# A decoder layer on one core: the last passes of the first feed-forward join the mixing stage's list schedule, which gets other costs and ranks

## The chip, the cores and the metric

The kernel runs on one core of a Trainium2 chip. Its time is the device time of one execution in microseconds (us). Before the change it is 2037.16 us, the median of three runs (2036.92 to 2037.41). The engines are named as in the profile: PE is TensorE's matmul, PEld its weight load, DVE is VectorE, ACT is ScalarE, POOL is GpSimd, and SP is SyncE, whose queue issues all the transfers.

## The reference, cut to what matters

16 meta tokens stand before 1024 tokens of width 1024. One layer is a first half-step feed-forward, a mixing stage, and a second half-step feed-forward; a norm closes it.

```python
h = h + 0.5 * swiglu(rmsnorm(h, norm_ffn1), w_ffn1_gate, w_ffn1_up, w_ffn1_down)   # d_ff = 2816
u = rmsnorm(h, norm_mix)
qa, ka, va, qi, ki, wi, qs, ksw, vsw, ga, gb = split(u @ w_in)      # rope on all q and k
score = sum_h relu(qi_h . ki) * wi_h                                # 4 index heads
o_sparse = softmax attention over each query's 256 best keys by score   # 8 heads, one k and v
o_swa = softmax attention over a window of 128 keys, with sinks         # 8 heads, two k and v
merged = sigmoid(ga) * (o_sparse @ w_bs) + sigmoid(gb) * (o_swa @ w_bw)
h = h + merged @ w_out
h = h + 0.5 * swiglu(rmsnorm(h, norm_ffn2), ...)
out = rmsnorm(h[tokens], norm_final)
```

## The kernel before, in words

Everything is held with the model width on the partitions and the tokens along the row, in two halves: half 0 has 528 columns (the meta tokens and 512 tokens), half 1 has 512. float32 products are made of float16 ones: each operand is split into a high and a low float16 part, and three matmuls are summed. A weight comes by a DMA into one of two staging buffers (`wst`), ACT writes its high part and DVE its low part into one of four buffers (`wsp`), and PE reads those. `split_w` is that pair of instructions.

A feed-forward works through the inner width in four groups. The first three groups, and the gate and up products of the fourth, are written out by hand with a fast scheme for 2 x 2 blocks. What is left, the down product of the fourth group, runs as two **plain passes**: for half 0 and then half 1, each of eight output rows `d` takes one weight, matmuls into the PSUM tile `pdn`, an addition into `h[d]` by DVE, a square by ACT (`sq`) and an addition into `acc` by DVE. After a pass, `norm_stats` (PE tile `nsum`, then a few DVE steps on `n_a`, `n_r`, `n_e`) and `norm_u` (PE tile `nbc`, then for each `d` the DVE product `un`, an ACT copy and a DVE subtraction, both into `u`) make the mixing stage's input. Half 0's norm is done during half 1's pass. `h` is also written out to DRAM, as `hspill`, to be read again at the end of the mixing stage.

The mixing stage is recorded and not executed at once: the class `Plan` collects its instructions, and `run` simulates the five queues with a cost per instruction and writes each engine's order out. At each step it takes the engine that can start first and, among that engine's ready instructions, the one with the lowest rank; the rank is the place in the recorded program plus `nc.shift`. The engines then execute that order strictly, each in its own queue, whatever the real durations are. The names in it: `rp` and `rt`, `ry` are the rope projections and their products; `kscr`, `qscr` are their way through DRAM into the stacked `k` and `q`; `pv_t` is the projection of the values; `ps_i`, `rel` and `sc1` to `sc7` are the index scores of the query blocks; `ps_s`, `psw`, `ptr`, `pts`, `pv_s`, `otr`, `oT` belong to the window attention; MAX8 and MATCH_REPLACE8 on `sc` and `m8` find the 256 best in blocks 1 to 4, and a binary search (`jk`, `s5...`) does so for blocks 5 to 7; `ps_a`, `psp`, `ptb`, `pv_b` are the sparse attention; `p_gate`, `p_br`, `gt`, `mg` the gates and branch products; `p_out` the output product.

Before the change the plan starts after the plain passes (`nc.start()` stands behind the call of `ffn`), so its first entries are half 1's norm and the rope projections. The cost of a DVE instruction in the plan depends on its width alone; a POOL instruction that runs beside it changes nothing.

Of the kernel before, what the change touches and what calls it, by code (L numbers as in the profile page):

```python
# [117 lines left out]
        return self.made  # L118


def overlap(a, b):
    return a is None or b is None or all(x0 < y1 and y0 < x1 for (x0, x1), (y0, y1) in zip(a, b))

# [9 lines left out]
class Plan:  # L133
# [48 lines left out]
    def add(self, engine, op, args, kw):  # L182
        if not self.on:
            give = lambda x: x.get() if isinstance(x, View) else x
            return getattr(engine.real, op)(*[give(a) for a in args], **{k: give(v) for k, v in kw.items()})  # L185
        outs = [a for a in args[:1]] + [kw[k] for k in ("out", "accum_out") if k in kw]
        ins = list(args[1:]) + [v for k, v in kw.items() if k not in ("out", "accum_out")]
        outs = [o for o in outs if isinstance(o, View)]
        ins = [o for o in ins if isinstance(o, View)]
        i = len(self.items)  # L190
        busy, done = self.cost(engine.name, op, outs, ins)
        if engine.name == "ACT" and "accum_out" in kw:
            busy, done = busy + 0.1, done + 0.19
        deps, new = set(), []
        for views, write in ((ins, False), (outs, True)):
            for v in views:
                b, box = v.base, v.box()
                for j, other, wrote in b.seen:
                    if (write or wrote) and j != i and overlap(box, other):
                        deps.add(j)  # L200
                if write and box is None:
                    b.seen = []
                b.seen.append((i, box, write))
                if b.first is None:
                    b.first = i
# [5 lines left out]
        self.items.append((engine, op, args, kw, busy, done, deps, new, i + self.shift))  # L211

    def start(self):
        self.on = True

    def run(self, keep=(), margin=0.25):
        items, names = self.items, ("PE", "DVE", "ACT", "POOL", "SP")
        count = len(items)
        kept = {id(t.base) for t in keep}
# [6 lines left out]
        for i, it in enumerate(items):  # L226
            for j in it[6]:
                users[j].append(i)
            waits[i] = len(it[6]) + len(it[7])
            for b in it[7]:  # L230
                queues.setdefault(b.key, []).append((i, b))
                free.setdefault(b.key, [0.0] * b.bufs)
# [13 lines left out]
        wire = [0.0]  # L246
        order, when = [], [0.0] * count

        def settle(i):
# [19 lines left out]
        while len(order) < count:  # L269
            best = None  # L270
            for e in names:
                while future[e] and future[e][0][0] <= clock[e]:
                    _, p, i = heapq.heappop(future[e])
                    heapq.heappush(now[e], (p, i))
                if now[e]:
                    t = clock[e]
                elif future[e]:
                    t = future[e][0][0]
                else:
                    continue  # L280
# [12 lines left out]
            order.append(i)  # L293
            for j in users[i]:
                f = items[j][0].name
                lag = 0.04 if f == e else 0.07 + (margin if f == "PE" else 0.0)
                at = t if f == e == "PE" else end + lag
                ready[j] = max(ready[j], at)
                waits[j] -= 1
                if not waits[j]:  # L300
                    settle(j)
            for b in dies[i]:
                if b.key in free:
                    free[b.key].append(end + 0.1)
                    grant(b.key)
# [26 lines left out]
def layer_kernel(ctx: ExitStack, tc: tile.TileContext, xT, gains, wgu1, wd1, win, wvi, wbs, wbw, wout,  # L332
# [24 lines left out]
        return new(big, [P, 528], F32, tag="nt", name=name, bufs=2)  # L357

    def tmp(shape, dt, name):
        return new(ph["sb"], shape, dt, tag="t", name=name, bufs=6)  # L360

    def atmp(shape, dt, name):
        return new(ph["sb"], shape, dt, tag="ta", name=name, bufs=2)

    def mcst(shape, dt, name, bufs=1):
        return new(ph["sb"], shape, dt, tag=name, name=name, bufs=bufs)
# [49 lines left out]
    def load_w(src, n, st=None):  # L416
        if st is None:
            st = load_raw(src, n)
        sp = wsp_tile()
        split_w(sp, st, n)  # L420
        return sp

    def mm3(ps, w, wcols, xt, xcols, start, stop):
# [49 lines left out]
        return res  # L473

    def fpage(shape, dt, name):
        return new(ph["sb"], shape, dt, tag="fp", name=name, bufs=27)

    def ftmp(name):
        return new(ph["sb"], [P, 528], F32, tag="ft", name=name, bufs=6)
# [23 lines left out]
                nc.scalar.activation(rb[:, s0:s1], ps[:, :w], AF.Copy)  # L503
        return (u, rb) if keep else u

    def ffn(u, rb, hs, gi, wgu, wd, other_half, passes, saved):
        S = ph["S"]
        wa = hs[0][0].shape[1] // S
        wb = 512 // S
# [7 lines left out]
        def new_hid(x):  # L517
            made[0] += 1
            shape = [P, 2, hs[x][0].shape[1]]
            if made[0] <= 11:  # L520
                return fpage(shape, F16, "hid")
            if made[0] <= 19:
# [301 lines left out]
        with tc.manual_schedule(engines=ORDERED):  # L824
            for f0, f1 in F_GROUPS:
# [23 lines left out]
                if not last:  # L849
                    for d in range(0, KD, 2):  # L850
                        fast_down(d, down)
        ready = None
        for x, subs, done in passes:
            c0, c1 = subs[0][0], subs[-1][1]
# [2 lines left out]
            for d in range(KD):  # L857
                nd = (f1 - f0) * P
                w = load_w(wd[d // 2][:, 2 * f0 * P + d % 2 * nd:2 * f0 * P + (d % 2 + 1) * nd], nd)
                ps = wide("pdn")  # L860
                if full:
                    plain(ps, w, [t[x] for t in hid], x)
# [44 lines left out]
    acc = ffn(u1, rb1, h, 0, wgu1, wd1, lambda: ffn1_norm(1),  # L907
              ((0, SUB_ALL[0], lambda r: mix_norm(0, r)), (1, SUB_ALL[1], None)), saved1)
    close_phase()
    open_phase("mix")  # L910
    nc.start()

    cos, sin = [], []
    for lst, i in ((cos, 0), (sin, 1)):
# [369 lines left out]
    for x in range(2):  # L1284
# [10 lines left out]
        for b in range(4 * x, 4 * x + 4):  # L1295
            swa_block(b, qs, oT_w[x])
    qa += q_groups((0, 1), 8, 2)

    vm_sp = v_meta(lambda hh: 0)
    oT_s = [new_oT()]  # L1300
# [102 lines left out]
    acc = ffn(u3, rb3, h2, 2, wgu2, wd2, lambda: ffn2_norm(1, acc), passes, saved2)  # L1403
    x, subs, done = passes[-1]
    done(norm_stats(acc, subs))
    close_phase()
# [91 lines left out]
```

## Time and profile before

| | us |
|---|---|
| median of three runs | 2037.16 |
| the profiled execution | 2036.95 |
| its span | 2035.0 |
| PE busy in the span | 1928.4 |
| DVE busy | 1627.0 |
| ACT busy | 900.8 |
| POOL busy | 385.7 |

The span has three parts that can be told apart in PE's rows: the first feed-forward to 637.89 us (the first matmul of the plain passes), the plain passes and the mixing stage to 1386.4 us, and the second feed-forward after that. An engine's busy time is a union: two instructions that overlap at their ends count once. The durations of single rows are a little longer than the distance from one start to the next, for the same reason. "PEclk" is the clock that TensorE was granted, as a share of 2.4 GHz.

### The profile page before, as it was taken

How to read it: one execution, taken by the hardware profiler on the slowest of the kernel's cores; microseconds unless marked ns; L12 is line 12 of the kernel's file. 1: busy time of each engine (PE TensorE's matmuls, PEld its weight loads, DVE VectorE, ACT ScalarE, POOL GpSimd, SP SyncE). 2: the span in 40 equal slices, each digit the busy share in tenths (PEclk: the TensorE clock that was granted, in tenths of full speed). 3: DMA queues.
4: the chain of work that ended last, by engine and by line, in shares of the span. 5: the costliest groups of instructions: out<-in, count | busy, mean ns of one | idle time of the engine just before them, and what ended most of it. 6: DMA issues, size and time to landing. Idle time of an engine off the chain costs nothing.

```text
span 2035.0 us, 32861 instructions
## 1 busy us (share of the span) xinstructions
PE 1928.4 (95%) x13080; PEld 1202.6 (59%) x13080; DVE 1627.0 (80%) x2779; ACT 900.8 (44%) x1602; POOL 385.7 (19%) x313
## 2 busy tenths in 40 slices
PE   5899999999999688889999999998899999999997
PEld 3488888888888354555555656444344444444443
DVE  7888788778875859999997977566988787788767
ACT  4433233333323434578888555443433243233232
POOL 3511312221310024122000000002312212312200
PEclk9899999999999799999999999999999999999998
DMA  4011111111113444321111232241112121111213
GB/s 158 11 63 48 58 63 51 55 63 58 48 63 101 135 142 140 95 84 58 34 46 33 74 103 73 83 156 52 32 57 65 46 75 49 63 62 47 76 39 129
DMA packets 58873, 146.95 MB, mean 72 GB/s; under 512 B 7264, under 2 KB 13408, under 8 KB 58720
## 3 DMA queue, kind: packets, MB, share of 16 engines
q1 hardware_dynamic: 58720, 144.86, 22.4%
q8 instruction: 102, 1.67, 0.3%
q14 instruction: 51, 0.42, 0.1%
HBM read 130.01 MB, written 14.76 MB: 71 GB/s over the span
## 4 chain that ended last, share of the span: by engine, by line
PE 75%; DVE 14%; ACT 5%; issue 3%; DMA 2%; POOL 1%; SPq 0%; DVEq 0%; ACTq 0%; POOLq 0%
PE pc L185 15%; PE pd L185 14%; PE pa L185 14%; PE pb L185 7%; PE p_gate L312 7%; PE p_out L312 4%; PE p_br L312 4%; PE pdn L185 3%; DVE sc L312 2%; PE ptr L312 2%; DVE u L185 1%; ACT psw L312 1%; PE pv_b L312 1%; PE rp L312 1%; ACT jk L312 1%
## 5 line engine op out<-in xcount | busy, mean ns | idle before, releaser
L185 PEld LDWEIGHTS <-wsp 128*128 128x128 f16 x5136 | 506.8, 99 | 312.0 <-issue 35.5
L185 PEld LDWEIGHTS <-x 128*128 128x128 f16 x3132 | 306.4, 98 | 156.4 <-issue 7.8
L312 PEld LDWEIGHTS <-wsp 128*128 128x128 f16 x2160 | 207.1, 98 | 205.6 <-ACT wsp L312 6.1
L185 PE MATMUL pa<-u,wsp 128*128 128x264 f16 (+1 forms) x1440 | 224.7, 310 | 0.0
L312 PE MATMUL p_gate<-u,wsp 128*128 128x512 f16 x768 | 187.3, 379 | 0.0
L185 POOL TENSOR_TENSOR h<-h,base 128x512 f32<-128x512 f32 (+1 forms) x72 | 116.3, 1616 | 291.1 <-DVE base L185 229.7
L185 ACT ACTIVATE wsp<-wst 128x1024 f16<-128x1024 f32 (+2 forms) x104 | 90.4, 870 | 165.8 <-DMA wst<-in_wd_dram 60.3
L312 PE MATMUL rp<-u,wsp 128*128 128x512 f16 (+2 forms) x624 | 143.4, 367 | 9.0 <-ACT wsp L312 5.8
L312 DVE SCALAR_TENSOR_TENSOR wsp<-wst,wsp 128x1024 f16<-128x1024 f32 (+1 forms) x88 | 98.1, 1116 | 32.9 <-ACT wsp L312 32.8
L185 PE MATMUL pb<-tb,wsp 128*128 128x264 f16 (+1 forms) x720 | 114.0, 312 | 7.9 <-ACT tb L185 5.7
L185 PE MATMUL pc<-tb,x 128*128 128x264 f16 (+1 forms) x720 | 112.3, 310 | 5.9 <-DVE c L185 5.7
L185 PE MATMUL pc<-tb,wsp 128*128 128x256 f16 (+1 forms) x720 | 114.8, 315 | 0.0
L312 ACT ACTIVATE wsp<-wst 128x1024 f16<-128x1024 f32 (+1 forms) x88 | 81.2, 928 | 70.1 <-PE p_out L312 23.7
L185 PE MATMUL pd<-u,x 128*128 128x256 f16 (+1 forms) x720 | 110.7, 308 | 0.0
L185 PE MATMUL pd<-tb,x 128*128 128x256 f16 (+1 forms) x720 | 110.7, 308 | 0.0
L185 DVE SCALAR_TENSOR_TENSOR wsp<-wst,wsp 128x1024 f16<-128x1024 f32 (+2 forms) x104 | 104.8, 1008 | 7.2 <-ACT wsp L185 7.1
L185 ACT ACTIVATE wsp<-sa 128x1024 f16<-128x1024 f32 (+1 forms) x64 | 62.3, 973 | 103.3 <-DVE sa L185 103.2
L185 POOL TENSOR_TENSOR t<-g,g 128x512 f32<-128x512 f32 x16 | 25.2, 1576 | 434.6 <-DVE g L185 434.6
L312 ACT ACTIVATE jk<-sc,s5nb 128x784 f16<-128x784 f32 (+2 forms) x93 | 98.4, 1058 | 16.0 <-DVE s5nb L312 13.5
L185 PE MATMUL pa<-hid,wsp 128*128 128x264 f16 (+1 forms) x648 | 103.1, 310 | 0.0
L185 PE MATMUL pd<-hid,x 128*128 128x256 f16 (+1 forms) x648 | 101.6, 308 | 0.0
L185 DVE TENSOR_TENSOR c<-pc,base 128x512 f32<-128x512 f32 x80 | 55.4, 692 | 51.6 <-PE pc L185 51.3
(215 smaller groups left out, 3442.3 us busy)
## 6 DMA issues: line engine op xcount, KB each, us to landing
wst<-in_wgu_dram SPq DMA_DIRECT2D x88, 512.0 KB, 3.9
wst<-in_win_dram SPq DMA_DIRECT2D x44, 512.0 KB, 3.5
wst<-in_wd_dram SPq DMA_DIRECT2D x48, 384.0 KB, 3.5
wst<-in_wd_dram SPq DMA_DIRECT2D x32, 256.0 KB, 2.7
wst<-in_wout_dram SPq DMA_DIRECT2D x16, 512.0 KB, 3.9
qscr<-ry SPq DMA_DIRECT2D x20, 256.0 KB, 2.1
q<-qscr SPq DMA_DIRECT2D x20, 256.0 KB, 3.1
wst<-in_wbs_dram SPq DMA_DIRECT2D x16, 256.0 KB, 2.9
```

The costliest lines, as they stand in the source:

```text
L185: return getattr(engine.real, op)(*[give(a) for a in args], **{k: give(v) for k, v in kw.items()})
L312: getattr(engine.real, op)(*[give(a) for a in args], **{k: give(v) for k, v in kw.items()})
```

## The change

Six things are edited. The plain passes of the first feed-forward are recorded into the plan (a callback, `to_mix`, closes the first phase, opens the mixing phase and starts the plan before the passes); in that form half 0 is two PSUM tiles, of 272 and 256 columns, and not one. The hidden tiles that the passes read move to a pool that outlives the phase and is shared with the mixing stage's temporary tiles. The plan adds 0.4 us to a DVE instruction that has two float32 inputs in SBUF and none in PSUM while a POOL instruction other than a copy is still running, and 1.3 us to an ACT instruction that needs another function table than the last. SP may start 6 us ahead of the plan's zero, and a transfer lands 0.5 us later in it. The weight splits get a rank that is 300 lower. And the projections of the window attention's queries are recorded between the index scores of two query blocks and those of the next two, those of the sparse attention's queries between and after the window blocks of half 1.

```diff
-    def run(self, keep=(), margin=0.25):
+    def run(self, keep=(), margin=0.25, early=0.0):
...
-            engine, op, args, kw, busy, done, deps, new, _ = items[i]
+            engine, op, args, kw, busy, done, deps, new, _, shared = items[i]
+            if e == "DVE" and shared and pool_till > t:
+                busy, done = busy + 0.4, done + 0.4
+            elif e == "ACT" and len(args) > 2 and args[2] in TABLES:
+                if TABLES[args[2]] != table:
+                    table = TABLES[args[2]]
+                    busy, done = busy + 1.3, done + 1.3
...
+            if e == "POOL" and op != "tensor_copy":
+                pool_till = end
...
-                end = wire[0] + 0.7
+                end = wire[0] + 1.2
...
         sp = wsp_tile()
+        nc.shift = -300
         split_w(sp, st, n)
+        nc.shift = 0
...
+        before_passes()
         ready = None
         for x, subs, done in passes:
...
+                if ph["mix"]:
+                    for a, b in subs:
+                        ps = mmps("pdn")[:, :b - a]
+                        proj(ps, w, [t[x] for t in hid], a, b)
+                        hv = hs[x][d][:, a:b]
+                        nc.vector.scalar_tensor_tensor(hv, ps, DS, hv, op0=ALU.mult, op1=ALU.add)
+                    square_into(d, hs[x][d], acc)
...
+                    if ready and d == 0:
+                        r = norm_stats(*ready[:2])
+                    if ready and d == 1:
+                        ready[2](r)
+                    continue
...
+    def to_mix():
+        close_phase()
+        open_phase("mix")
+        nc.start()
...
-        for b in range(4 * x, 4 * x + 4):
-            if b:
-                score(b)
-        qs += q_groups((x,), 4, 2)
...
+        first = 4 * x
+        scores((first, first + 1))
+        half = q_groups((x,), 4, 1)
+        scores((first + 2, first + 3))
+        qs.append(half[0] + q_groups((x,), 6, 1)[0])
...
-    nc.run(h2[0] + h2[1] + u3[0] + rb3 + [acc])
+    nc.run(early=6.0, keep=h2[0] + h2[1] + u3[0] + rb3 + [acc])
```

The instructions themselves stay the same but for the narrower pieces of half 0; what changes is the order. Three places show it. The first is PE at the end of the plain passes (`pdn` of `h[7]` of half 1 is the last piece of them; `nsum` and `nbc` are half 1's norm; `rp1` is the first rope projection of half 0). Before:

```order
L185 MATMUL pdn_7647<-hid_7100,wsp_7644 128x512
L312 MATMUL nsum_7674<-ones_97,acc_7384 128x1 x4
L312 MATMUL nbc_7717<-ident_93,n_r_7701 128x128 x4
L312 LDWEIGHTS wsp_7754
L312 MATMUL rp1_7761<-u_7445,wsp_7754 128x272
```

and now:

```order
L326 LDWEIGHTS wsp_7629
L326 MATMUL pdn_7669<-hid_7100,wsp_7629 128x512
L326 LDWEIGHTS wsp_7674
L326 MATMUL rp1_7693<-u_7534,wsp_7674 128x272
L326 LDWEIGHTS wsp_7674
```

Half 1's norm no longer stands between the passes and the rope projection; its `nsum` now comes behind four further projections. The second place is DVE at the same point: the low part of the first rope weight (`wsp_7754` before, `wsp_7674` now). Before it comes behind six products of half 1's norm (`un` of `h_77` to `h_82`):

```order
L312 SCALAR_TENSOR_TENSOR un_7725<-h_77,g_all_95,nbc_7717 128x512
L312 SCALAR_TENSOR_TENSOR un_7728<-h_78,g_all_95,nbc_7717 128x512
L312 TENSOR_TENSOR u_7731<-un_7725,u_7731 128x512
...
L312 SCALAR_TENSOR_TENSOR un_7756<-h_82,g_all_95,nbc_7717 128x512
L312 SCALAR_TENSOR_TENSOR wsp_7754<-wst_7711,wsp_7754 128x1024
```

and now it comes before the last addition of the passes (`h_84`), while half 1's `acc` additions follow among the rope products:

```order
L326 SCALAR_TENSOR_TENSOR wsp_7674<-wst_7619,wsp_7674 128x1024
...
L326 SCALAR_TENSOR_TENSOR h_84<-pdn_7669,h_84 128x512
L326 SCALAR_TENSOR_TENSOR wsp_7702<-wst_7650,wsp_7702 128x1024
...
L326 SCALAR_TENSOR_TENSOR wsp_7766<-wst_7697,wsp_7766 128x1024
L326 TENSOR_TENSOR acc_7477<-acc_7477,sq_7779 128x512
L326 TENSOR_TENSOR rt2_7805<-rp2_7733,cs_7137 128x272
```

So the weight's split has moved ahead of half 1's norm, and the norm's DVE work has moved behind the first rope products. The third place is SP's queue ahead of the plain passes (`wd1` holds their weights, `wgu1` the last gate and up weights). Before, six weights of the passes stand in a row:

```order
L185 DMA wst_6611<-in_wgu1_dram 128x1024
L185 DMA wst_7112<-in_wd1_dram 128x512
L185 DMA wst_7146<-in_wd1_dram 128x512
L185 DMA wst_7180<-in_wd1_dram 128x512
L185 DMA wst_7214<-in_wd1_dram 128x512
L185 DMA wst_7248<-in_wd1_dram 128x512
```

and now the masks stand behind the second:

```order
L188 DMA wst_6611<-in_wgu1_dram 128x1024
L326 DMA wst_7125<-in_wd1_dram 128x512
L326 DMA wst_7131<-in_wd1_dram 128x512
L326 DMA msk0_7141<-in_m_swa0_dram 128x144
L326 DMA msk1_7143<-in_m_swa_dram 128x256
L326 DMA sp0_7145<-in_m_sp0_dram 128x144
L326 DMA snk_7147<-in_sinks_dram 128x8
L326 DMA wst_7160<-in_wd1_dram 128x512
```

The mask's transfer goes into memory of the closed phase, so it waits for the last DVE instruction of that phase, and the third weight stands behind it.

## Rows read from the trace of the kernel before

**Rows 1.** The page's first part: busy time of each engine, share, instructions.

```profile
PE 1928.4 (95%) x13080; PEld 1202.6 (59%) x13080; DVE 1627.0 (80%) x2779; ACT 900.8 (44%) x1602; POOL 385.7 (19%) x313
```

**Rows 2.** Windows: busy us and instructions by engine, then PEclk, DMA share, GB/s.

```profile
637.89:688.00 50.11, 46.64 (x310) 30.47 (x307) 40.13 (x81) 24.14 (x47) 0.11 (x1) 0.97 0.54 176
688.00:706.00 18.00, 5.08 (x21) 4.11 (x22) 12.99 (x29) 7.46 (x12) 0.84 (x1) 0.59 0.10 30
706.00:748.00 42.00, 37.14 (x281) 26.00 (x281) 21.28 (x38) 12.61 (x21) 12.15 (x12) 0.97 0.50 159
748.00:945.00 197.00, 178.00 (x1367) 105.32 (x1366) 187.49 (x468) 119.61 (x298) 51.40 (x38) 0.99 0.30 98
945.00:1386.40 441.40, 437.71 (x3043) 237.68 (x3042) 350.81 (x857) 280.52 (x544) 18.49 (x68) 1.00 0.24 76
1386.40:1450.00 63.60, 53.89 (x235) 24.92 (x235) 52.78 (x65) 27.21 (x41) 25.67 (x17) 0.92 0.09 25
```

**Rows 3.** Chain that ended last, 684 to 706: start, us, what.

```profile
687.82 0.69 DVE h L185
...
691.60 0.70 DVE acc L185
...
692.43 1.85 PE nsum L312 x8
...
695.76 2.09 PE nbc L312 x8
...
704.69 1.15 DVE wsp L312
```

**Rows 4.** PE's timeline: start, us, instruction, idle before it and its releaser.

```profile
632.57 2.86 PE L185 MATMUL pc<-tb,x 128*128 128x264 f16 x24
635.27 2.78 PE L185 MATMUL pd<-u,x 128*128 128x256 f16 x24
...
664.30 2.75 PE L185 MATMUL pdn<-hid,wsp 128*128 128x512 f16 x12
666.89 1.28 PE L185 MATMUL nbc<-ident,n_r 128*128 128x16 f32 x10
...
705.89 12.36 PE L312 MATMUL rp<-u,wsp 128*128 128x272 f16 x94 [1.17 <-DVE wsp L312]
720.29 10.10 PE L312 MATMUL rp<-u,wsp 128*128 128x512 f16 x46 [2.04 <-DVE wsp L312]
...
747.79 0.41 PE L312 MATMUL ps_i<-k,q 128*128 128x272 f16 x2 [0.51 <-DMA q<-qscr]
```

**Rows 5.** Chain that ended last, 636 to 664: start, us, what.

```profile
639.50 0.63 DVE hid L185
...
647.37 3.03 DMA wst<-in_wd_dram
...
650.49 0.64 ACT wsp L185
...
651.87 4.90 DMA wst<-in_wd_dram
```

**Rows 6.** DVE's groups by form, 640 to 706: busy us, mean ns, idle before.

```profile
L185 DVE SCALAR_TENSOR_TENSOR wsp<-wst,wsp 128x512 f16<-128x512 f32 x12 | 8.3, 689 | 3.7 <-ACT wsp L185 3.6
...
L312 DVE SCALAR_TENSOR_TENSOR un<-h,g_all,nbc 128x512 f32<-128x512 f32 x6 | 4.2, 742 | 2.2 <-PE nbc L312 2.2
...
L312 DVE TENSOR_TENSOR u<-un,u 128x512 f16<-128x512 f32 x5 | 3.4, 690 | 0.0
...
L312 DVE SCALAR_TENSOR_TENSOR wsp<-wst,wsp 128x1024 f16<-128x1024 f32 x1 | 1.2, 1218 | 0.0
```

**Rows 7.** DVE's groups, 748 to 945, the two of the search for the best.

```profile
L312 DVE MAX8 m<-sc 128x8 f32<-128x400 f32 (+3 forms) x40 | 24.7, 634 | 0.0
L312 DVE MATCH_REPLACE8 sc<-m,sc 128x400 f32<-128x400 f32 (+3 forms) x39 | 24.2, 620 | 0.0
```

**Rows 8.** DVE's timeline at 760 us.

```profile
760.68 1.35 DVE L312 TENSOR_SCALAR sc<-rel,wi 128x256 f32<-128x256 f32 x1
```

**Rows 9.** DVE's groups by form, 700 to 960.

```profile
L312 DVE TENSOR_SCALAR sc<-rel,wi 128x352 f32<-128x352 f32 x2 | 0.8, 387 | 0.0
```

More of the change, by code (lines that the diff above doesn't have):

```diff
@@ L118, in real @@
         return self.made
+TABLES = {AF.Sqrt: 0, AF.Silu: 1, AF.Exp: 2, AF.Tanh: 2, AF.Sign: 2}
 def overlap(a, b):
@@ L210, in add @@
                 b.last = i
-        self.items.append((engine, op, args, kw, busy, done, deps, new, i + self.shift))
+        shared = sum(v.dt == F32 and not v.base.whole for v in ins) > 1 and not any(v.base.whole for v in ins)
+        self.items.append((engine, op, args, kw, busy, done, deps, new, i + self.shift, shared))
     def start(self):
         self.on = True
-    def run(self, keep=(), margin=0.25):
+    def run(self, keep=(), margin=0.25, early=0.0):
         items, names = self.items, ("PE", "DVE", "ACT", "POOL", "SP")
@@ L231, in run @@
                 queues.setdefault(b.key, []).append((i, b))
-                free.setdefault(b.key, [0.0] * b.bufs)
+                free.setdefault(b.key, [-early] * b.bufs)
                 tiles[id(b)] = b
@@ L245, in run @@
         clock = dict.fromkeys(names, 0.0)
-        wire = [0.0]
+        clock["SP"] = -early
+        wire = [-early]
+        pool_till, table = 0.0, None
         order, when = [], [0.0] * count
@@ L359, in tmp @@
     def tmp(shape, dt, name):
-        return new(ph["sb"], shape, dt, tag="t", name=name, bufs=6)
-    def atmp(shape, dt, name):
-        return new(ph["sb"], shape, dt, tag="ta", name=name, bufs=2)
+        return new(big, shape, dt, tag="late", name=name, bufs=8)
+    atmp = tmp
     def mcst(shape, dt, name, bufs=1):
@@ L475, in fpage @@
     def fpage(shape, dt, name):
-        return new(ph["sb"], shape, dt, tag="fp", name=name, bufs=27)
+        return new(ph["sb"], shape, dt, tag="fp", name=name, bufs=19)
     def ftmp(name):
@@ L504, in norm_u, with ffn @@
         return (u, rb) if keep else u
-    def ffn(u, rb, hs, gi, wgu, wd, other_half, passes, saved):
+    def ffn(u, rb, hs, gi, wgu, wd, other_half, passes, saved, before_passes):
         S = ph["S"]
@@ L519, in new_hid @@
             shape = [P, 2, hs[x][0].shape[1]]
+            if made[0] <= 8:
+                return tmp(shape, F16, "hid")
             if made[0] <= 11:
@@ L859, in ffn @@
                 w = load_w(wd[d // 2][:, 2 * f0 * P + d % 2 * nd:2 * f0 * P + (d % 2 + 1) * nd], nd)
+                if ph["mix"]:
[5 more added lines that the diff above has]
+                    square_into(d, hs[x][d], acc)
+                    if d == 0:
+                        warm = small(1, "n_warm")
+                        nc.scalar.activation(warm, acc[:, :1], AF.Sqrt)
+                    if ready and d == 0:
[3 more added lines that the diff above has]
+                    continue
                 ps = wide("pdn")
@@ L905, in mix_norm @@
             nc.sync.dma_start(hsp[k][:, HS0[x]:HS0[x + 1]], h[x][k])
+    def to_mix():
+        close_phase()
+        open_phase("mix")
+        nc.start()
     acc = ffn(u1, rb1, h, 0, wgu1, wd1, lambda: ffn1_norm(1),
[L908 to L911, printed above, removed]
+              ((0, SUB_ALL[0], lambda r: mix_norm(0, r)), (1, SUB_ALL[1], None)), saved1, to_mix)
     cos, sin = [], []
@@ L1289, in layer_kernel, with scores @@
         v_half(x)
-        for b in range(4 * x, 4 * x + 4):
-            if b:
-                score(b)
-        qs += q_groups((x,), 4, 2)
+        def scores(bs):
+            for b in bs:
+                if b:
+                    score(b)
+        first = 4 * x
[3 more added lines that the diff above has]
+        qs.append(half[0] + q_groups((x,), 6, 1)[0])
         oT_w.append(new_oT())
-        for b in range(4 * x, 4 * x + 4):
+        for b in range(first, first + 2):
             swa_block(b, qs, oT_w[x])
-    qa += q_groups((0, 1), 8, 2)
+        if x == 1:
+            late = q_groups((0, 1), 8, 1)
+        for b in range(first + 2, first + 4):
+            swa_block(b, qs, oT_w[x])
+    qa += [a + b for a, b in zip(late, q_groups((0, 1), 10, 1))]
     vm_sp = v_meta(lambda hh: 0)
@@ L1402, in layer_kernel @@
     passes = [last_pass(0, 0, 512), last_pass(1, 0, 512)]
-    acc = ffn(u3, rb3, h2, 2, wgu2, wd2, lambda: ffn2_norm(1, acc), passes, saved2)
+    acc = ffn(u3, rb3, h2, 2, wgu2, wd2, lambda: ffn2_norm(1, acc), passes, saved2, lambda: None)
     x, subs, done = passes[-1]
```

## The prediction

> **What bounds the kernel now.** I read the page's busy times first: PE is busy 1928.4 of 2035.0 us [rows 1], so a change that moves work without removing any can win at most the rest, about 107 us, and only where PE stands idle. The windows say where that is [rows 2]. Between the end of the first feed-forward's fast products (637.89) and the end of the mixing stage (1386.40) PE idles 3.5 us in the plain passes, 12.9 of the 18 us behind them, 4.9 in the rope projections, 19.0 between the first index score (748) and the first sparse scores (945), and 3.7 in the 441 us after that. That is 44 us. The idle time before 637.89, and that after 1386.40, lies in stretches whose order the change does not touch, so I leave it as it is.
>
> Each of these stretches has another limit. In 688 to 706 it is a chain with nothing beside it, which the chain of waits shows [rows 3]: the last addition into `h` (687.82), the additions into `acc` to 692.3, `nsum`, the small steps, `nbc` at 695.76, half 1's norm on DVE, and behind it the low part of the first rope weight at 704.69. PE's granted clock there is 0.59, between the two levels of 2.4 and 1.2 GHz, after it had stood idle; in the stretches around it is 0.97. From 748 to 945 DVE is busy 187.5 of 197 us, 95%, and PE 178.0: both are near their limit, DVE nearer. After 945 PE is the bound: 437.7 of 441.4, with DVE at 350.8.
>
> **The change, part by part.**
>
> *Passes to the first rope projection.* PE's work in it: 24 matmuls of 264 columns come every 2.70 us (the distance of the two starts [rows 4]), so half 0's eight rows are 21.6 us (the 272 and 256 columns are the same sum); half 1's are 8 x 2.6 = 20.8 by the distance of 664.30 and 666.89; half 0's `nsum` and `nbc` some 2.4 (1.28 for the second). Sum 44.8. New stalls come in at the start. Before, six weights were ready ahead of the passes; now the low part of the first one stands on DVE behind the last hidden tile, which ends at 640.13 [rows 5], and takes 0.69 [rows 6]: PE can run four matmuls and waits from 638.4 to about 641.0, 2.6 us. The third weight's transfer waits for the same DVE instruction, behind four mask transfers; it lands about 3 us later [rows 5], and its high part stands on ACT behind the square of the second row, its low part on DVE behind that row's `acc`: PE's second row ends at 641.0 + 44 x 0.11 = 645.9 (four of its and the first row's 48 are done before); its addition takes 0.4 more, the square about 0.6, the high part 0.64, so 647.5, and `acc` and the low part 0.69 each from 646.9, so 648.3. PE has six matmuls of 0.11 for the time between: 2.3 us of stall, estimated. Later weights come in time by the same walk (the fifth at 652.9, just when PE gets to it). So 44.8 + 4.9 = 49.7, and the first rope projection at about 688. DVE allows it: it was busy 40.1 in this window, and now six `acc` additions leave it and two splits of 1.2 us enter. Half 1's norm no longer lies on the way. Before, the projection began in earnest at 705.89 [rows 4]: **minus 18 us**. Bounds: minus 12 if the weights of the passes come late throughout (one more us on every other one), minus 20 if the start costs nothing.
>
> *Rope projections to the first index score.* 705.89 to 747.79 is 41.9 us now. Seven more rope matmuls (0.22 each, from 46 in 10.10 [rows 4]) and half 1's `nsum` and `nbc` come in, 1.5 + 2.4; about 1.1 of slow clock goes (0.97 of 37 us); of the 4.9 idle I expect 2.5 to stay, since `qscr` now stands ahead of all but one of the eight small `vm` transfers. 42.4: **no change**. The cover for half 1's norm is here: 8 `un` and 8 `u` of 0.74 and 0.69 and six `acc` make 15.6 us [rows 6], of which 3.5 lay in this window already. DVE was busy 21.3 of 42 [rows 2], so 34.5 fits. If it did not, the scores would start later by what is left over: up to 6 us.
>
> *Scores and window attention, 748 to 945.* The same work, ordered by a plan that sees DVE slower. Ahead of the first sparse row on DVE stood 40 pairs of MAX8 and MATCH_REPLACE8, and in the new order there are 34: six pairs of 1.22 us (busy time over count [rows 7]) leave the stretch that DVE bounds, 7.3 us, and go to the one after it, where DVE has 90 us free. At the same 95% this is **minus 7.7 us**. Also about 3 us of PE work (transposes and products of the last window block) moves behind the border: **plus 3 us** there. Bounds for the stretch: no gain at all (the pairs filled time in which DVE waited), and minus 19.0, all of PE's idle time.
>
> *The costs in the plan.* The 0.4 us are no time in themselves; they make the plan's clock for DVE later, which is what shifts those pairs. GpSimd's drag is in the trace: a TENSOR_SCALAR of 256 columns takes 1.35 us at 760.68, with rope work on POOL beside it [rows 8], and one of 352 columns 0.39 elsewhere [rows 9]. The new rule leaves this instruction out: it has one float32 input. The Trainium skill (SBUF — State Buffer, Who interferes with whom) says that single-input forms such as `tensor_scalar` take the port shared with GpSimd in their two-port modes, and then wait for the whole of the other's instruction. The row agrees. By that rule the plan still misjudges a part of DVE's delays; the third rival below says what this would do.
>
> *The rest.* The rope tables and masks leave the crowded transfers of 637 to 688; half 0's narrower tiles add eight DVE additions (16 of half the width for 8), about 0.1 us each. The rank of the splits keeps PE from waiting for weights (1.2 and 2.0 us in rows 4); I count that in the 2.5 above.
>
> Sum: -18 + 0 - 7.7 + 3 = -22.7. The profiled execution is 2036.95, so 2014.3; the median of the runs is 0.2 above that execution. **Predicted: 2014 us.**
>
> **The rivals.**
>
> *DVE takes it back* (2027). Half 1's norm now runs beside the rope's POOL work; if each of its 22 instructions is dragged by 0.4, DVE needs 34.5 + 9 = 43.5 of 42 us, the scores start 6 us late, and the shorter stretch is not had: -18 + 6 + 3 = -9. For it: POOL is busy 12.2 us in that window. Against: 20.7 us of DVE are free in it.
>
> *The whole idle time goes* (2003). If the new order also lets PE run through most of 748 to 945, with 5 of 19.0 us left: -18 - 14 - 2 = -34. For it: PE's waits there are short and many. Against: DVE at 95%.
>
> *The drag is counted at the wrong instructions* (2022). If delays that the plan leaves out decide the stretch, its length stays 197, and only the first step is had: -18 + 3 = -15. For it: a single-input form is dragged by about 1 us, and the plan doesn't count it [rows 8, 9]. The rule of the Trainium skill quoted above says the same. Against: fewer pairs stand in DVE's way whoever drags it.
>
> *Slower: SP's queue* (2046). Place: the weights of the plain passes. A weight takes 3.0 to 4.9 us to land, 0.64 for its high and 0.69 for its low part [rows 5, 6]: 4.4 to 6.2. With two under way this is 2.2 to 3.1 for each, about PE's 2.7; but each now stands behind an `hspill` that waits for the addition before it. If that leaves one under way at a time, each of 14 weights costs PE up to 3.5 more. From 1.6 more on each the gain is eaten; at 2.3 on each, 32 us: 2046. Against: the spills stood between the weights before as well, and PE idled only 3.5 us.
>
> *It does nothing* (2037): PE has the same work, and what is won at 688 is lost where the scores wait for `q`. PE's work between would have to find no DVE time; rows 2 speak against it.
>
> **How the numbers follow.** My forecast, with its own range of 2008 to 2020, has 0.50; the drag at the wrong instructions 0.16; DVE taking it back 0.15; the whole idle time 0.09; nothing 0.04; slower 0.06. A measurement of this kernel tells 0.2%, 4 us, from no change. Faster: 0.50 + 0.16 + 0.15 + 0.09 = 0.90; within 0.2% 0.04; slower 0.06. The range of 2003 to 2028 takes in the first four cases: 2003 is the bound of the stretch, 2028 the first rival.
>
> **What would show it.** Right: no gap in PE between the last `pdn` and the first `rp`, with the first `rp` at 686 to 691; PEclk near 1 there; PE waiting 2 to 3 us for `wsp` at 638 and again at 646; the first `ps_i` near 730; DVE still above 93% busy from there to the first `psp`, which comes at about 919; PE above 99% after that. Wrong: first `rp` after 695 (the passes starve for weights); first `ps_i` after 736 (DVE takes it back); a stretch from `ps_i` to `psp` as long as 197 us or longer; or new idle time on PE behind `psp`, which the six deferred pairs could cause.

## The result and the profile after

The changed kernel takes 2009.01 us (median of 4 runs, 2007.83 to 2010.08); the kernel before, beside it, 2037.29 (2036.92 to 2038.47). The ratio is 0.9861, 95% interval 0.9845 to 0.9876: 28.3 us faster. 2014 was forecast, 2003 to 2028 as the range. The time and the sign came out; the reason given for one of the two large terms did not, and the two large terms missed in opposite directions, so that the closeness of the total is partly luck.

The page's busy line of the changed kernel, whose span is 2007.3 us, answers to [rows 1].

```profile
PE 1922.9 (96%) x13080; PEld 1201.4 (60%) x13080; DVE 1630.3 (81%) x2787; ACT 898.2 (45%) x1602; POOL 385.1 (19%) x313
```

PE's busy time is down 5.5 us for as many matmuls; the other 22 us of the span were PE's idle time. The windows of the changed kernel say where it went (columns as in [rows 2]). Their borders are events: first `pdn` of the passes, first `rp`, first `ps_i`, first `psp` on DVE, first matmul of the second feed-forward. The fifth line is a piece of the first.

```profile
638.07:691.53 53.46, 48.02 (x308) 31.17 (x308) 39.02 (x86) 22.12 (x43) 0.95 (x1) 0.94 0.52 168
691.53:733.80 42.27, 39.52 (x307) 28.27 (x306) 37.95 (x70) 21.93 (x39) 13.97 (x12) 1.00 0.54 167
733.80:915.70 181.90, 169.90 (x1294) 101.48 (x1293) 179.28 (x446) 111.16 (x280) 49.37 (x39) 0.99 0.33 107
915.70:1360.10 444.40, 441.51 (x3112) 241.18 (x3110) 363.94 (x886) 288.23 (x564) 17.89 (x67) 1.00 0.24 76
640.00:650.00 10.00, 7.75 (x44) 5.42 (x44) 4.07 (x13) 2.13 (x3) 0.95 (x1) 0.66 0.36 109
```

Against the events of before (637.89, 705.89, 747.79 and 1387.0 on PE, 945.1 on DVE), with the term of the sum beside each:

| part | before | after | difference | predicted |
|---|---|---|---|---|
| passes to first `rp` | 68.0 | 53.5 | -14.5 | -18 |
| `rp` to first `ps_i` | 41.9 | 42.3 | +0.4 | 0 |
| first `ps_i` to first `psp` | 197.3 | 181.9 | -15.4 | -7.7 |
| first `psp` to the second feed-forward | 441.9 | 444.4 | +2.5 | +3 |
| sum | | | -27.0 | -22.7 |

The first two lines need a word: 705.89 is the point from which the prediction counted, but before it, at 703.65, PE had already run the first four `rp` matmuls. From the first `rp` itself the two parts are 65.8 and 44.1 us before, and the differences -12.3 and -1.9; their sum stays the same. The last 0.8 us fall in the second feed-forward, whose order the change does not touch.

The parts are those of one profiled execution of each kernel. The executions of one kernel lie up to 6.5 us apart (2020.87 to 2027.35 for "only the passes" below, whose profiled one is the longest), so a difference of a microsecond or two between parts says little.

PE's timeline of the changed kernel answers to [rows 4] (start, length, instruction, idle time before it and its releaser).

```profile
638.07 0.61 PE L326 MATMUL pdn<-hid,wsp 128*128 128x272 f16 x4 [0.78 <-DVE base L188]
642.00 7.75 PE L326 MATMUL pdn<-hid,wsp 128*128 128x272 f16 x44 [3.31 <-DVE wsp L326]
651.46 19.49 PE L326 MATMUL pdn<-hid,wsp 128*128 128x272 f16 x157 [1.71 <-ACT wsp L326]
670.79 1.17 PE L326 MATMUL nsum<-ones,acc 128*128 128x1 f32 x10
671.83 2.53 PE L326 MATMUL pdn<-hid,wsp 128*128 128x512 f16 x11
674.78 1.38 PE L326 MATMUL nbc<-ident,n_r 128*128 128x16 f32 x10 [0.42 <-DVE n_r L326]
675.99 15.70 PE L326 MATMUL pdn<-hid,wsp 128*128 128x512 f16 x72
691.53 0.40 PE L326 MATMUL rp<-u,wsp 128*128 128x272 f16 x2
...
733.80 0.40 PE L326 MATMUL ps_i<-k,q 128*128 128x272 f16 x2
```

The bare chain of [rows 3] is gone: the last `pdn` run reaches up to the first `rp`. In its place stand the two waits for `wsp` that were forecast, 3.31 and 1.71 us, before 642.00 and 651.46. A third wait, 0.78 us for `base`, stands just ahead of the first `pdn` and so outside the table; before the change there was none. What the first split stands behind shows on DVE:

```profile
640.50 0.68 DVE L188 TENSOR_TENSOR hid<-g,hid 128x512 f16<-128x512 f32 x1
...
641.25 0.68 DVE L326 SCALAR_TENSOR_TENSOR wsp<-wst,wsp 128x512 f16<-128x512 f32 x1
```

DVE's groups from 733.8 to 915.7 answer to [rows 7], and the last line to [rows 8, 9] (form and count, busy us, mean ns, idle time before).

```profile
L326 DVE MAX8 m<-sc 128x8 f32<-128x400 f32 (+3 forms) x34 | 20.7, 620 | 0.0
L326 DVE MATCH_REPLACE8 sc<-m,sc 128x400 f32<-128x400 f32 (+3 forms) x33 | 20.0, 608 | 0.0
L326 DVE TENSOR_SCALAR sc<-rel,wi 128x336 f32<-128x336 f32 (+8 forms) x11 | 6.3, 576 | 0.0
```

Six pairs fewer, as read from the order, and 8.2 us less DVE time in them. DVE is busy 98.6% of the stretch where it had been 95%. It all looks like the forecast mechanism with a larger size. The experiments show that it is not.

Last, what PE waited for in this stretch: first the kernel before, 747.8 to 945.1, then the changed one, 733.8 to 915.7 (us in total, times, longest).

```profile
PE ps_i L312 <- ACT rel L312: 5.0, 7, 1.2
PE ps_s L312 <- DMA q<-qscr: 3.2, 3, 1.6
PE pv_s L312 <- ACT pts L312: 3.1, 6, 0.8
PE pv_t L312 <- DVE vt L312: 2.7, 1, 2.7
PE ps_s L312 <- DVE a_mx L312: 2.3, 4, 1.1
```

```profile
PE ps_s L326 <- DVE a_mx L326: 3.4, 5, 1.1
PE rp L326 <- DVE rt L326: 3.4, 2, 2.1
PE ps_i L326 <- ACT rel L326: 2.4, 7, 0.8
PE pv_s L326 <- ACT pts L326: 2.1, 5, 0.6
```

Before, PE idled 19.0 us in 27 short waits; now 12.0 in 21. The waits for `q` (3.2) and in the middle for `vt` (2.7) are gone, that of the scores for `rel` is half as long, and one for `rt` (3.4) is new.

### The profile page after: what moved, and what is told of

Read it like the earlier page. It is cut to its first block, busy times and chain, and to the rows that moved or that the text cites. A ratio compares the mean times of both kernels' runs of the same rounds, so it can differ in the third digit from the quotient of the medians.

```text
span 2007.3 us, 32840 instructions
## 1 busy us (share of the span) xinstructions
PE 1922.9 (96%) x13080; PEld 1201.4 (60%) x13080; DVE 1630.3 (81%) x2787; ACT 898.2 (45%) x1602; POOL 385.1 (19%) x313
## 4 chain that ended last, share of the span: by engine, by line
PE 79%; DVE 12%; ACT 5%; issue 2%; DMA 1%; POOL 1%; SPq 0%; DVEq 0%; ACTq 0%; POOLq 0%
PE pc L188 15%; PE pd L188 15%; PE pa L188 15%; PE pb L188 7%; PE p_gate L326 7%; PE p_out L326 4%; PE p_br L326 3%; PE pdn L188 2%; PE ptr L326 2%; PE rp L326 2%; ACT jk L326 1%; PE pdn L326 1%; PE pv_b L326 1%; DVE wsp L326 1%; DVE sc L326 1%
## 5 line engine op out<-in xcount | busy, mean ns | idle before, releaser
L188 ACT ACTIVATE wsp<-wst 128x1024 f16<-128x1024 f32 (+2 forms) x88 | 80.4, 915 | 142.3 <-DMA wst<-in_wd_dram 50.4
L326 ACT ACTIVATE wsp<-wst 128x1024 f16<-128x1024 f32 (+2 forms) x104 | 91.1, 880 | 58.4 <-PE p_out L326 16.4
L188 POOL TENSOR_TENSOR t<-g,g 128x512 f32<-128x512 f32 x16 | 25.5, 1592 | 434.4 <-DVE g L188 434.4
L188 ACT ACTIVATE base<-pa 128x528 f32<-128x528 f32 (+1 forms) x64 | 38.2, 598 | 133.6 <-PE pa L188 133.6
```

## The experiments

All twelve beside each other. Passes, rope, stretch and behind are the four parts of the table above, in us; PE idle, DVE idle and pairs are those of the stretch. The ratio is to the kernel before, which was run beside each group (medians 2036.4 to 2037.4). All rows count from the first `rp` matmul, the kernel before too.

| kernel | passes | rope | stretch | behind | PE idle | DVE idle | pairs | median | ratio, interval |
|---|---|---|---|---|---|---|---|---|---|
| before | 65.8 | 44.1 | 197.3 | 441.9 | 19.0 | 9.7 | 40 | 2037.3 | 1 |
| after | 53.5 | 42.3 | 181.9 | 444.4 | 12.0 | 2.6 | 34 | 2009.0 | 0.9861 (0.9845-0.9876) |
| only the passes | 53.6 | 47.5 | 194.5 | 442.0 | 17.7 | 2.9 | 45 | 2023.6 | 0.9933 (0.9915-0.9952) |
| plan's costs and rank only | 65.1 | 45.2 | 189.3 | 441.7 | 16.3 | 6.9 | 39 | 2025.6 | 0.9946 (0.9926-0.9966) |
| no drag | 53.3 | 46.4 | 184.6 | 445.3 | 15.4 | 2.2 | 40 | 2014.3 | 0.9887 (0.9872-0.9902) |
| old place of projections | 53.4 | 41.9 | 193.4 | 440.8 | 17.8 | 7.0 | 38 | 2016.2 | 0.9898 (0.9883-0.9913) |
| no rank | 60.0 | 44.6 | 189.6 | 448.2 | 18.0 | 11.5 | 33 | 2028.0 | 0.9953 (0.9938-0.9968) |
| wider drag | 53.8 | 42.6 | 184.7 | 445.0 | 17.0 | 4.9 | 34 | 2013.0 | 0.9886 (0.9870-0.9903) |
| pairs of 3, 4 held back | 52.2 | 43.6 | 185.5 | 459.0 | 14.2 | 15.2 | 20 | 2025.2 | 0.9941 (0.9926-0.9955) |
| pairs of 2, 3, 4 held back | 53.7 | 41.9 | 182.0 | 476.7 | 10.7 | 30.6 | 2 | 2040.6 | 1.0019 (1.0009-1.0028) |
| lag 0.26 | 52.5 | 43.3 | 187.9 | 443.5 | 15.3 | 8.2 | 33 | 2012.0 | 0.9881 (0.9859-0.9903) |
| four weights ahead | 45.9 | 43.1 | 186.4 | 443.3 | 15.3 | 7.9 | 33 | 2004.7 | 0.9840 (0.9824-0.9855) |
| four ahead, wider drag | 45.8 | 43.0 | 185.9 | 446.3 | 17.1 | 3.6 | 34 | 2005.9 | 0.9847 (0.9833-0.9862) |
| four ahead, pairs of 3, 4 held back | 45.9 | 43.1 | 184.5 | 459.0 | 14.6 | 15.0 | 20 | 2019.0 | 0.9909 (0.9892-0.9925) |

Some of the expectations quoted below give 179.2 us as the length of the changed kernel's stretch, with 2.4 us of DVE idle; that is up to the first `p_gate`, 2.7 us before the first `psp`. The table goes to `psp` throughout.

**The two halves of the change.** Only the passes join the plan:

```
-            if e == "DVE" and shared and pool_till > t:
+            if False:
-            elif e == "ACT" and len(args) > 2 and args[2] in TABLES:
+            elif False:
-                end = wire[0] + 1.2
+                end = wire[0] + 0.7
-        nc.shift = -300
-        nc.shift = 0
... (projections at their old place, no early=6.0)
```

> The plain passes join the plan; the drag, the table cost, SP's head start, the rank of the splits and the moved projections are all taken back. Theory (the gap behind the passes and the scoring stretch are two separate gains): only the gap is won, first rp about 14.5 us earlier relative to the first pdn, the stretch from the first ps_i to the first p_gate stays near 193 us, so 2022 to 2024. Rival 1 (the passes alone make the whole gain, the stretch is shorter because it begins with VectorE less behind): stretch near 180 us, 2009. Rival 2 (the gap is won only with the other edits): 2035.

And the plan's new costs and the rank without passes and without moved projections:

```
-               ((0, SUB_ALL[0], lambda r: mix_norm(0, r)), (1, SUB_ALL[1], None)), saved1, to_mix)
+               ((0, SUB_ALL[0], lambda r: mix_norm(0, r)), (1, SUB_ALL[1], None)), saved1, lambda: None)
+    to_mix()
... (projections at their old place)
```

> The passes stay out of the plan and the projections stand where they stood before; the drag, the table cost, SP's head start and the rank of the splits are in. Theory (two separate gains): the gap stays at 18 us, the stretch from the first ps_i to the first p_gate is some 5 to 12 us shorter than before's 193.5, so 2025 to 2032. Rival 1 (passes alone): 2037. Rival 2 (the costs are what matters everywhere): 2015.

Both came out as the theory had it: -13.7 and -11.8 us of the medians, together 25.5 of 28.3. So the gain in front and most of the gain in the stretch are two things. The passes alone keep a stretch of 194.5; the costs and the rank alone leave the passes where they were (65.1).

**The drag taken out of the plan.**

```
-            if e == "DVE" and shared and pool_till > t:
+            if False:
```

> The changed kernel without the 0.4 us in the plan; 40 pairs of MAX8 and MATCH_REPLACE8 stand ahead of the first sparse row again, as before, where the change has 34. Theory of the prediction (the pairs in VectorE's way are what shortened the stretch): 7 to 9 us slower than the change, 2016 to 2018, stretch near 187. Rival (VectorE's lost waits, not the pairs, made the gain, and they come from the moved projections or the rank): 2009 to 2011, stretch near 180, VectorE still 98% busy.

It costs 5.3 us, between the two. Forty pairs stand ahead again, and 2.7 us of the loss are in the stretch, 4.1 in the rope part. Six pairs by 1.2 us would be 7.3.

**The projections at their old place.**

```
-        scores((first, first + 1))
-        half = q_groups((x,), 4, 1)
-        scores((first + 2, first + 3))
-        qs.append(half[0] + q_groups((x,), 6, 1)[0])
+        scores(range(4 * x, 4 * x + 4))
+        qs += q_groups((x,), 4, 2)
...
-    qa += [a + b for a, b in zip(late, q_groups((0, 1), 10, 1))]
+    qa += q_groups((0, 1), 8, 2)
```

> The changed kernel with one part undone: the sliding-window projections stand again behind all four index-score blocks of a batch, not among them; passes, drag, costs and ranks stay as changed. DVE now has 38 pairs of MAX8 and MATCH_REPLACE8 ahead of the first psp, where the changed kernel has 34. Theory (the place of the projections decides how many pairs stand in the stretch that DVE bounds): 4 pairs of 1.2 us more, and some of DVE's 2.4 us of idle time grows, so the stretch from first ps_i to first psp grows from 179.2 to 183 to 186 us, and the median comes to 2013 to 2016. Rival (the gain of the stretch came from drag and passes, the projections' place is worth nothing): 179 to 181 us, 2008 to 2011.

2016.2, just above what the theory allowed, but with 11.5 us more in the stretch, and four pairs are 4.9. What PE waits for there, 733.3 to 926.7, names the rest:

```profile
PE ps_i L326 <- ACT rel L326: 6.2, 11, 1.5
PE ps_s L326 <- DVE a_mx L326: 5.2, 5, 2.6
...
PE ps_s L326 <- DMA q<-qscr: 0.9, 1, 0.9
```

With the projections in one piece PE waits for ACT's `rel` 6.2 us, not 2.4; that it has less to put between two scores is the likely reason, which no run shows by itself. Of the 11.5 us, 3.6 are work that moved to this side of the border: the part behind is that much shorter (440.8).

**The rank taken out.**

```
-        nc.shift = -300
         split_w(sp, st, n)
-        nc.shift = 0
```

> The changed kernel with one part undone: the weight splits keep the rank of their product, without the 300 that brought them forward; all else as changed. 33 pairs stand ahead of the first psp, 34 in the changed kernel. Theory (PE's short waits for wsp come back, DVE bounds the stretch either way): PE waits for wsp grow from 5 us to 8 to 10 us between 637 and 915, the stretch from first ps_i to first psp stays within 179 to 182, the median 2009 to 2013. Rival (the rank is what brought DVE's idle time down from 9.7 to 2.4 us): DVE idles 6 us or more in that stretch, 184 us or longer, the median 2014 to 2017.

The largest loss of the three parts undone alone, 19.0 us, and more than either side had. Both were right in part, and the parts add up. DVE idles 11.5 us in the stretch and PE 18.0, as the rival said. PE's waits for `wsp` grow to 9.7 us, as the theory said, but all in the passes, which lose 6.5. DVE's timeline there, then PE's:

```profile
677.20 0.69 DVE L326 SCALAR_TENSOR_TENSOR wsp<-wst,wsp 128x512 f16<-128x512 f32 x1
677.80 0.79 DVE L326 TENSOR_TENSOR u<-un,u 128x272 f16<-128x272 f32 x2
678.51 0.90 DVE L326 SCALAR_TENSOR_TENSOR un<-h,g_all,nbc 128x272 f32<-128x272 f32 x2
...
684.83 0.87 DVE L326 SCALAR_TENSOR_TENSOR un<-h,g_all,nbc 128x256 f32<-128x256 f32 x2
685.61 0.69 DVE L326 SCALAR_TENSOR_TENSOR wsp<-wst,wsp 128x512 f16<-128x512 f32 x1
```

```profile
686.36 6.61 PE L326 MATMUL pdn<-hid,wsp 128*128 128x512 f16 x22 [2.77 <-DVE wsp L326]
694.86 2.33 PE L326 MATMUL pdn<-hid,wsp 128*128 128x512 f16 x10 [1.89 <-DVE wsp L326]
```

Half 0's norm (`un`, `u`) runs beside half 1's pass, and without the rank 7.8 us of DVE's work, most of it that norm, go ahead of a split of 0.69 that PE stands waiting for. The 4.7 us of added waiting cost the passes 6.5. With the passes alone the rank was out too, and they took 53.6: in these runs it is needed with the other costs, not by itself.

**More of the drag counted**, the third rival of the prediction.

```
-        shared = sum(v.dt == F32 and not v.base.whole for v in ins) > 1 and not any(v.base.whole for v in ins)
+        shared = op.startswith("tensor_scalar") and len(outs) == 1 and len(ins) and not ins[0].base.whole or sum(not v.base.whole and v.shape[-1] > 8 for v in ins) > 1
```

> The changed kernel with a wider rule: the 0.4 us is counted also for tensor_scalar forms with one SBUF tensor and for splits with one float32 and one bfloat16 input, which the changed kernel leaves out. 34 pairs ahead of the first psp as in the changed kernel. Rival of the prediction (the drag is counted at the wrong instructions, delays left out decide the stretch): a stretch of 174 to 177 us instead of 179.2, the median 2003 to 2007. Theory (DVE is busy 98.6% of that stretch, so no order of the same 34 pairs can shorten it by more than 2.4 us): 178 to 181 us, the median 2007 to 2011.

2013.0 (2010.0 to 2015.3): not faster. The stretch is 2.8 us longer with the same 34 pairs. The rival falls, and the theory's 2007 to 2011 was too low.

**The pairs held back.** This is the test of the third term itself: if a pair costs its 1.2 us ahead of `psp`, fewer pairs make a shorter stretch.

```
-        deps, new = set(), []
+        deps, new = set() if self.gate is None else {self.gate}, []
...
+    border = len(nc.items) - 1
     vm_sp = v_meta(lambda hh: 0)
...
+    nc.gate = border
     by_max(3)
+    nc.gate = None
... (the same around by_max(4))
```

> The changed kernel with one edit to the plan: the MAX8 and MATCH_REPLACE8 pairs of blocks 3 and 4 may not be placed before the last projection in front of the sparse attention. 20 pairs stand ahead of the first psp, where the changed kernel has 34. Theory (each pair costs its 1.2 us in a stretch that DVE bounds): 14 pairs are 17 us, more than stands between DVE's 176.8 us and PE's 167.2, so PE becomes the bound; from the first ps_i to the first psp 168 to 174 us, where the changed kernel takes 181.9; the pairs run behind it, where DVE has 80 us free; the median 2000 to 2004. Rival (the plan places pairs only where DVE would wait, so they cost nothing): 180 to 183 us with DVE idle 15 us or more, the median 2008 to 2014.

And with the same lines around `by_max(2)` as well:

> The same edit for the pairs of blocks 2, 3 and 4: 2 pairs stand ahead of the first psp. Theory: the stretch is PE's already with 20 pairs, so it is no shorter, 168 to 174 us from the first ps_i to the first psp; behind it the third sparse row waits for 18 pairs, 22 us of DVE, which other work of PE covers in part: the median 2000 to 2008. Rival (pairs cost nothing ahead of the first psp): 180 to 183 us, and what is deferred is late: the median 2012 to 2025.

My theory falls. The rival's stretch came out with 2 pairs (182.0) and nearly with 20 (185.5 for 180 to 183), but both medians lie above the rival's ranges too. The windows of the stretch and of the part behind it, first with 20 pairs ahead, then with 2:

```profile
732.80:918.30 185.50, 171.27 (x1351) 103.61 (x1350) 170.28 (x420) 126.24 (x315) 49.94 (x38) 1.00 0.33 105
918.30:1377.30 459.00, 443.27 (x3059) 241.74 (x3056) 376.15 (x911) 275.51 (x529) 19.50 (x68) 0.99 0.23 73
```

```profile
733.80:915.80 182.00, 171.35 (x1354) 104.22 (x1353) 151.45 (x366) 127.87 (x316) 48.96 (x38) 0.99 0.33 106
915.80:1392.50 476.70, 443.18 (x3050) 241.49 (x3049) 394.23 (x965) 275.94 (x528) 19.54 (x68) 0.97 0.23 71
```

With 2 pairs DVE is busy 151.5 of 182.0 us, and the stretch is as long as with 34 (181.9). Twenty-eight microseconds of DVE's work were taken out and the stretch is no shorter; at most 1.5 us came back, as more work of PE's in the same time (171.4 us busy for 169.9). What was held back is late behind the border; PE's waits there, with 20 pairs and with 2:

```profile
PE ps_a L326 <- DVE b_mx L326: 7.2, 4, 4.6
PE p_gate L326 <- DVE wsp L326: 2.7, 1, 2.7
```

```profile
PE ps_a L326 <- DVE b_mx L326: 28.0, 4, 24.1
```

So the pairs are filler in this stretch: taking them out shortens nothing. This was tried in the changed kernel only; for the kernel before, with its 40 pairs, it is an inference. DVE's 80 free us behind the border were no cover for them, since a sparse row of PE's waits for its pairs at one place.

**A change of order that means nothing.** One constant of the plan, the lag that it counts before a PE instruction, from 0.25 to 0.26 us:

```
-    def run(self, keep=(), margin=0.25, early=0.0):
+    def run(self, keep=(), margin=0.26, early=0.0):
```

> The changed kernel with one number of the plan moved by 0.01 us: the lag that it counts before a PE instruction, 0.25 to 0.26. Nothing of the change is undone; the plan only comes out in another order, with 33 pairs ahead of the first psp. Theory (the stretch is set by many short waits of PE, whose sum depends on which order the plan happens to find): PE idles 12 to 18 us from the first ps_i to the first p_gate, where it idles 12.0 in the changed kernel, and the median lies 2 to 7 us above the changed kernel's, 2011 to 2016. Rival (the changed costs and ranks set the gain, small changes of order are worth nothing): idle time within 1.5 us of 12.0, the median 2007 to 2011.

2012.0 (2010.4 to 2014.7), PE idle 15.3 us: the theory's case, though its interval of the ratio overlaps that of the changed kernel. Some 3 us of the median is therefore what another order of the same work can be worth here, by this one trial, and more in the stretch alone: it is 187.9 us, 6.0 longer, with one pair fewer. The 5.3 of the drag and the 4.0 of the wider drag are little above 3; neither can be put down to the 0.4 us as such.

**The start of the passes.** The first four weights are loaded and split ahead of them:

```
+        ahead = [load_w(wd[d // 2][:, 2 * f0 * P + d % 2 * nd:2 * f0 * P + (d % 2 + 1) * nd], nd)
+                 for d in range(4 if S == 2 else 0)]
         before_passes()
...
-                w = load_w(wd[d // 2][:, 2 * f0 * P + d % 2 * nd:2 * f0 * P + (d % 2 + 1) * nd], nd)
+                w = ahead.pop(0) if ahead else load_w(
```

> The changed kernel with the first four weights of the plain passes loaded and split ahead of the plan, as before the change; the masks then stand behind six of the weights in SP's queue. Theory (the 5.8 us of idle PE and the slow clock at 638 to 651 are lost to the late splits and the masks in the queue): first rp 5 to 7 us earlier relative to the first pdn, 2002 to 2004. Rival (VectorE sets the time of the second pass anyway): first rp at most 2 us earlier, 2007 to 2009.

The windows of its passes and its stretch:

```profile
637.40:683.30 45.90, 45.25 (x309) 30.32 (x308) 36.75 (x82) 21.66 (x40) 0.95 (x1) 1.00 0.57 175
726.40:912.80 186.40, 171.12 (x1311) 102.94 (x1311) 178.51 (x450) 119.77 (x300) 50.75 (x39) 0.99 0.31 100
```

The passes win 7.6 us: 4.8 of idle time, and 2.8 of PE's busy time, with the clock at 1.00 where it was 0.94. The stretch gives 4.5 back, in part to its longer PE idle time (15.3). At 2004.7 us (2003.6 to 2006.0) this is the fastest kernel of the study: its slowest execution is faster than the fastest of the changed kernel (2007.8), though the intervals of the two ratios overlap a little. Two attempts to keep what it gives back, with the wider drag and with the pairs held back:

> The wider rule of the drag together with the first four weights of the passes loaded and split ahead of them. With those four weights alone the first rp came 45.9 us after the first pdn, not 53.4, and the stretch from first ps_i to first psp took 181.7 us, not 179.2: DVE idled 7.1 us in it, not 2.4. Theory (the two are independent: passes 46 us; the stretch 178 to 182): median 2002 to 2005. Rival (counting DVE's delays more fully takes the idle time out of the stretch here as it did in the changed kernel): stretch 175 to 178, median 1998 to 2002.

> The pairs of blocks 3 and 4 held back and the first four weights of the passes loaded and split ahead of them. Theory (the two gains add up): 46 us from the first pdn to the first rp, 168 to 174 us from the first ps_i to the first psp, the median 1995 to 2000. Rival (what the earlier start gives is lost in the stretch behind it): the median 2001 to 2006.

The first stays at 2005.9, above its theory; the second is slower by 14 us, all of it behind the border (459.0), as without the four weights.

## Why the prediction was right, and where not

*Passes, -14.5 for -18: the mechanism held, one size was off.* The two stalls, estimated at 4.9 us, were 5.02, but that sum is luck. The first was 3.31 for 2.6: the hidden tile of [rows 5] that ends at 640.13 is not the last one, and in the changed kernel the last ends at 641.18. The second was 1.71 for 2.3: its own terms, 648.3 less 645.9 and less six matmuls of 0.11, give 1.7; it came at 649.75, not 646, behind the slow matmuls. PE's work, 44.8 in the sum, was 48.0 busy. The 44 matmuls behind the first stall took 7.75 us; by the 2.70 us for 24 that the sum used they are 4.95. In 640 to 650, of which the first 2.0 us are still the wait, the granted clock was 0.66, between its two levels of 2.4 and 1.2 GHz. The step priced the stalls and left out the slow matmuls behind them, 2.8 us, though the same sight stood in [rows 2]: 0.59 in 688 to 706. This price is not fixed: behind the same wait the 44 matmuls took 6.48 us with 20 pairs ahead and 8.03 with the wider drag. With four weights ahead both go at once, and 45.25 us of work are left.

*Rope part, +0.4 for 0.* Right, on the prediction's own count from 705.89. DVE is busy 38.0 of 42.3 us there, more than the 34.5 of the prediction (whose own terms, 21.3 + 15.6 - 3.5, give 33.4), and still does not make the scores late; the first rival (2027) is out. The first `ps_i` came at 733.8, not 730, for the 3.5 us of the passes.

*The stretch, -15.4 for -7.7: the step that failed.* That six pairs of 1.22 us "leave the stretch that DVE bounds" and shorten it by their length is refuted: with 32 pairs fewer still, the stretch has the same length. DVE did not bound it in the changed kernel. Its high share was made of work that must run and of pairs that fill what is left. The prediction named this among its bounds ("the pairs filled time in which DVE waited") and priced it at no gain; the gain came from elsewhere. What the windows and waits show in its place is PE's own work and its short waits on chains through ACT, DVE and the `qscr` transfer. Of the 15.4 us, 7.0 are PE's idle time (19.0 to 12.0) and 8.4 its busy time, of which 3.9 reappear behind the border with the 68 matmuls that moved there. The remaining 4.5 are less busy time over both parts (4412 and 4406 records). Six rope matmuls fewer are some 1.3 of it, at 0.22 each: they now run ahead of the first `ps_i`. The window's transposes (`ptr` of `psw`, 120 in both) take 18.6 us for 20.4. What made those and the rest shorter stays open; no run asked. The result lies within the bounds given for the stretch, 0 and -19, but not for the reason of either, since only 7.0 of it are idle time. And another order alone moves this length by 6.0, so a part of the 15.4 may be a lucky order.

*Which edit did it.* No single one. Undone alone, each of three lengthens the stretch: the drag by 2.7, the rank by 7.7, the place of the projections by 11.5, with PE idle 15.4 to 18.0 us. Against the 6.0 us of the lag, which undoes nothing, the first is nothing and the second little. By the medians the rank is worth 19.0 and the place of the projections 7.2, against 3.0 of the lag. The costs and the rank without the rest reach 189.3. The prediction gave the rank no term of its own and the projections none; these two are the larger ones, and only the rank stands far above what another order does. The table loads' price, the earlier start and the later landing were not tried alone.

*Behind it, +2.5 for +3.* Right in size. PE is at 99.3% there.

*The rivals.* That the whole idle time goes (2003) was half true: its reason, that the order lets PE run through, is what happened, to 12 us and not to 5. The drag at the wrong instructions (2022) is out. The Trainium skill (SBUF — State Buffer, Who interferes with whom) says that single-input forms, in their two-port modes, wait for the whole of an instruction of GpSimd's that came first. The traces agree: of the 11 TENSOR_SCALAR on `rel` and `wi`, four ran beside a POOL instruction before the change and took 1.03 to 1.47 us, the other seven 0.35 to 0.44; in the changed kernel two did, with 1.41 and 1.46, and nine took 0.34 to 0.44. One of the two, and the POOL instruction that ends 0.2 us before it does:

```profile
833.18 1.41 DVE L326 TENSOR_SCALAR sc<-rel,wi 128x384 f32<-128x384 f32 x1
832.94 1.43 POOL L326 TENSOR_TENSOR rt<-rt,rt 128x512 f32<-128x512 f32 x1 [38.68 <-PE ps_i L326]
```

But a plan that counts them too is not faster. SP's queue (2046) did not come up: after 651 no weight of the passes is late.

## What to carry to other kernels

A high busy share does not make an engine the bound when a list schedule fills it with work that nobody waits for yet: hold the filler back, as here, and see whether the time moves, then look at what the other engine waits for. Price a stall with the slow matmuls behind it; here taking out 4.8 us of waiting gave 7.6. And before a few microseconds are credited to a planner's rule, move a constant that means nothing: here 0.01 us in one lag moved the median by 3 and one stretch by 6.

## What had not been expected of the hardware

After a PE wait of 3.31 us, which ended at 642.00, the granted clock over 640 to 650 was 0.66, and 44 matmuls took 7.75 us for 4.95. With the four weights ahead and no such wait the clock was 1.00 over the whole of the passes.
